# Streamed weight tiles moved by 64 bytes, and the dense layers rewritten in 256-column products

## Chip, cores and metric

The kernel runs on one core of one Trainium2 chip. The metric is the device time of one execution in microseconds (us). The median of three runs of the kernel before is 2948.8 us (2945.6 to 2950.67).

## What is computed

Two transformer blocks over 256 tokens of width 2048, in float32. Cut to what matters here:

```python
# first block
h = rmsnorm(x); proj = h @ w_in                      # 2048 -> 9264
y_a = y_pool @ w_pool_out;  y_b = (o_nsa * silu(g)) @ w_nsa_out
gm = sigmoid(h @ w_merge + b)
x = x + (gm[0] * y_a + gm[1] * y_b) @ w_out
# second block
z = rmsnorm(x) @ w_in_2                              # 2048 -> 6160
x = x + mixed @ w_out_2
# peer_ffn: 16384 experts, 8 heads of 16 chosen ones
q = xt @ w_q; idx, gate = top16(scores(q))
y = sum_k gelu(u[idx_k] . xt) * gate_k * v[idx_k]
```

The kernel computes the expert layer densely: it multiplies all 16384 rows of u with the tokens, multiplies the result by a matrix of gates that is zero for experts not chosen, and multiplies that by all of v. So every weight, 554 MB in all, is streamed through once.

## The kernel before, in words

Every large weight comes in blocks of 128 partitions x 1024 float32 (512 KB). `stream` (L178 is its DMA) loads a block into a ring tile wr, then `split` makes two float32r tiles of it: wh, a rounded copy, by ScalarE (L156), and wl, the remainder, by VectorE (L157). A product of full precision is then three products of parts: high x high, high x low and low x high. The activations are kept in the same way, in tiles S0 to S5 (class Parts): for each of 16 slices of 128 rows, 256 columns of high part and then 256 of low part, 2048 bytes.

TensorE does four kinds of large work, in this order in time:

- **Dense layers, weights stationary** (`dense_half`, 360 blocks, to 1372 us). A block holds eight slices k. For each, one 512-column product of wh with both parts of the activations (L209) writes 512 columns of PSUM, and one 256-column product of wl with the high part (L211; L208 at the end of a layer) is summed into the second half of those. A layer output of 128 rows is two blocks and takes a whole PSUM bank; its two halves are summed when it is taken out: `two_sums` copies the first half by ScalarE (L228) and adds the second by VectorE (L229). `pair_T` does this for two outputs and then multiplies by the norm's factor on GpSimd (L224). The three mm banks (`mmtile`) rotate.
- **Dense layers, weights moving** (`dense_N`, tile mmn, 64 blocks of 12 products of 512 columns, L190 to L192), between the former.
- **The expert layer up** (`dense_pair`, L1142, from 1386 to 2226 us). For 256 blocks of peer_u and 24 of w_pq, each block is 24 products of 256 columns, weights stationary, all summed into one place: eight of wh with the high part, eight of wh with the low part, eight of wl with the high part. After each block `work` issues small jobs from a list: the choice of experts (products sc) and, from about 1700 us, the gate matrix (products G, L1264).
- **The expert layer down** (`v_mm`, L1333 and L1337, from 2226 us). 256 blocks of peer_v, each 12 products of 512 columns, the streamed block moving and the gated activations ah and al stationary.

Where the tiles lie. Pools are laid out one behind the other in each partition. In the memory map of the kernel before, the constants start at a multiple of 128 bytes and take 5376 = 42 x 128 bytes, so the ring tiles wr, wh, wl of the pool "stream" (4096 bytes each) all start at a multiple of 128, and so do the S tiles (16640 = 130 x 128 bytes). Call such a tile aligned. The tile ypp (activations of w_po) starts 64 bytes past a multiple of 128, call that shifted. In the expert layer a second pool "stream2" is open, whose tiles are shifted, and so are ah and al. There `stream` takes wh and wl from stream2 for two blocks in five:

```python
        pl, nb = (more[0], more[2]) if more and turn[1] % 5 in (1, 3) else (ws, NHL)
```

In the pattern of five, then, blocks go shifted, aligned, shifted, aligned, aligned. S0 and S3 hold the activations of the expert layer up, S0 and S1 those of the first `dense_N`; S0, S2, S3 lie below 113 KB and S1, S4, S5 above, as stream2 does.

The order on each engine is that of a list scheduler in the tile framework, which works from the program's order and priorities. All weight DMAs are issued on SyncE's queue.

Of the kernel before, what the change touches and what calls it, by code (L numbers as in the profile page):

```python
# [7 lines left out]
F32 = mybir.dt.float32  # L8
F32R = mybir.dt.float32r
I32 = mybir.dt.int32  # L10
U32 = mybir.dt.uint32
AF = mybir.ActivationFunctionType
# [3 lines left out]
P = 128  # L16
T = 256
# [113 lines left out]
def emit(tc, I, out):  # L131
    nc = tc.nc
    ve, se, te, dma = nc.vector, nc.scalar, nc.tensor, nc.sync.dma_start
    mult, add, sub, amax = ALU.mult, ALU.add, ALU.subtract, ALU.max
    es = ExitStack()

    def pool(stack, name, bufs=1, psum=False, **kw):
        if psum:
            kw["space"] = bass.MemoryType.PSUM
        return stack.enter_context(tc.tile_pool(name=name, bufs=bufs, **kw))  # L140

    cp = pool(es, "const")
    ws = pool(es, "stream")

    def const(key, pl=None):
        ap = I[key]
        t = (pl or cp).tile(list(ap.shape), F32, name="k_" + key)
        dma(t, ap)
        return t
# [25 lines left out]
    def stream(src):  # L175
        n = src.shape[-1]
        r = raw_tile()
        dma(r[:, :n], src)  # L178
        turn[1] += 1
        pl, nb = (more[0], more[2]) if more and turn[1] % 5 in (1, 3) else (ws, NHL)  # L180
        h = pl.tile([P, 1024], F32R, tag="wh", bufs=nb, name="wh")
        l = pl.tile([P, 1024], F32R, tag="wl", bufs=nb, name="wl")
        on_pool[2] += 1
        eng = nc.gpsimd if on_pool[2] % on_pool[1] < on_pool[0] else ve
        split(r[:, :n], h[:, :n], l[:, :n], eng)
        return h, l
# [9 lines left out]
    def mmtile(name="mm"):  # L196
        return mm_pool[0].tile([P, 512], F32, tag="mm", bufs=mm_pool[1], name=name)
# [3 lines left out]
    def dense_half(pt, w, n, hf, x, start, stop):  # L201

        h, l = first.pop() if first else stream(w[n, hf])
        for k in range(8):
            kk, s = hf * 8 + k, slice(k * P, k * P + P)
            last = stop and k == 7
            if last:
                te.matmul(pt[:, T:], l[:, s], x.hi(kk), start=False, stop=False, skip_group_check=True)  # L208
            te.matmul(pt, h[:, s], x.both(kk), start=start and k == 0, stop=last, skip_group_check=True)  # L209
            if not last:  # L210
                te.matmul(pt[:, T:], l[:, s], x.hi(kk), start=False, stop=False, skip_group_check=True)  # L211
        if between:
            f, c = between.pop(0)
            f(c)

    def pair_T(dst, w, n2, x, r=None, nh=2):

        for a in range(2):
            pt = mmtile()
            for hf in range(nh):  # L220
                dense_half(pt, w, 2 * n2 + a, hf, x, hf == 0, hf == nh - 1)
            two_sums(dst[:, a], pt)
        if r is not None:
            nc.gpsimd.tensor_tensor(dst, dst, two(r), op=mult)  # L224
        return dst

    def two_sums(dst, pt):
        se.activation(dst, pt[:, :T], AF.Copy)  # L228
        ve.tensor_tensor(dst, dst, pt[:, T:], op=add)  # L229

    def dense_N(w, n, x):

# [10 lines left out]
    def two(r):  # L243
        return r[:, None, :].to_broadcast([r.shape[0], 2, T])

    sy = pool(es, "sy")
    es_x = ExitStack()
    sx = pool(es_x, "sx")
    SW = 4160
# [249 lines left out]
    pt = cmp_start("k")  # L499
# [3 lines left out]
    pt = cmp_start("v")  # L503
# [11 lines left out]
    h, l = stream(I["w_gb"])  # L515
    for k in range(KC):
        s = slice(48 * k, 48 * k + 48)
# [127 lines left out]

    es_m = ExitStack()
    pm = pool(es_m, "pm")
    ypp = Parts(pm.tile([P, 16 * T], F32R, name="ypp"))
    e8 = slice(0, 8)
    split(yp, ypp.hi(e8), ypp.lo(e8))  # L650
    on = parts(2, 4)
# [3 lines left out]
    mg = parts(5, 3)  # L655
    for n2 in range(8):
        g0, g1 = g0s[n2], g1s[n2]
        for g, w, x, nh in ((g0, "w_po", ypp, 1), (g1, "w_no", on, 2)):
            b = pair_T(pm.tile([P, 2, T], F32, tag="br", bufs=2, name="br"), I[w], n2, x, nh=nh)
            ve.scalar_tensor_tensor(g, g, 1.0, b, op0=add, op1=mult)  # L660
        ve.tensor_tensor(g0, g0, g1, op=add)
        ns = slice(2 * n2, 2 * n2 + 2)
        split_scaled(g0, 0.5, mg.hi(ns), mg.lo(ns))
        if n2 < 5:
            gate_pair(n2 + 3)
# [17 lines left out]
    pm = pool(es_m, "pm2")  # L683
# [3 lines left out]
    xr = act3(big(0, F32))  # L687
    for c in range(4):
        dma(xr[:, 4 * c:4 * c + 4], I["xT"][:, 4 * c:4 * c + 4])
    x1 = act3(big(1, F32))  # L690
# [1 line left out]
    acc1 = pm.tile([P, 2, T], F32, name="acc1")  # L692
    acc2 = pm.tile([P, 2, T], F32, name="acc2")
    for n2 in range(8):
        xs = pair_T(x1[:, 2 * n2:2 * n2 + 2], I["w_o"], n2, mg)
        nc.gpsimd.tensor_tensor(xs, xs, xr[:, 2 * n2:2 * n2 + 2], op=add)
        s1 = acc1 if n2 == 0 else pm.tile([P, 2, T], F32, tag="s1", bufs=2, name="s1")
        s2_ = acc2 if n2 == 0 else pm.tile([P, 2, T], F32, tag="s2", bufs=2, name="s2")
        for a in range(2):
            c = 2 * n2 + a  # L700
            split_scaled(xs[:, a], fn1[:, c:c + 1], zn.hi(c), zn.lo(c))
        se.activation(s1, xs, AF.Square)
        for a in range(2):
            c = 2 * n2 + a
            se.activation(s2_[:, a], xs[:, a], AF.Square, scale=fnw[:, c:c + 1])
        if n2:
            ve.tensor_tensor(acc1, acc1, s1, op=add)
            ve.tensor_tensor(acc2, acc2, s2_, op=add)
# [337 lines left out]

    def out_half(c, hf):
        if hf == 0:
            vs_[c] = mmtile()
        dense_half(vs_[c], I["w_o2"], c, hf, mx_, hf == 0, hf == 1)  # L1050

    for c in range(3):
# [1 line left out]
    for n2 in range(8):  # L1054
        xs = x1[:, 2 * n2:2 * n2 + 2]
        for c in (2 * n2, 2 * n2 + 1):
            if c > 2:
                out_half(c, 0)
            out_half(c, 1)
            v, xc = vs_.pop(c), x1[:, c]  # L1060
            for i in range(2):
                ve.tensor_tensor(xc, xc, v[:, T * i:T * i + T], op=add)
            split_scaled(xc, n2w[:, c:c + 1], x2.hi(c), x2.lo(c))
        s1 = acc3 if n2 == 0 else pc.tile([P, 2, T], F32, tag="s1", bufs=2, name="s1")
        se.activation(s1, xs, AF.Square)
        if n2:
            ve.tensor_tensor(acc3, acc3, s1, op=add)
        if n2 >= 2:
            to_rows(n2 - 2)
# [61 lines left out]
            f()  # L1131

    def dense_pair(pt, w, n2, rate):

        for a in range(2):
            o = pt[:, T * a:T * a + T]
            for hf in range(2):
                h, l = stream(w[2 * n2 + a, hf])
                for i in range(3):
                    for k in range(8):  # L1140
                        kk, s = hf * 8 + k, slice(k * P, k * P + P)
                        te.matmul(o, (l if i == 2 else h)[:, s], x2s.lo(kk) if i == 1 else x2s.hi(kk),  # L1142
                                  start=hf == 0 and i == 0 and k == 0, stop=hf == 1 and i == 2 and k == 7,
                                  skip_group_check=True)
                work(rate)

    def top16(src, vals, idx):
# [272 lines left out]
```

## Time and profile before

| | |
|---|---|
| median of three runs | 2948.8 us |
| the profiled execution, its own time | 2948.61 us |
| its span, first to last instruction | 2946.8 us |
| PE (TensorE matmul) busy | 2902.4 us, 98%, 17810 products |
| DVE (VectorE) busy | 1971.2 us, 67% |
| ACT (ScalarE) busy | 1595.7 us, 54% |
| POOL (GpSimd) busy | 152.2 us, 5% |
| mean DMA traffic | 202 GB/s |
| mean granted TensorE clock | 0.996 of 2.4 GHz |

How to read it: products are pipelined, so a product of 256 columns is shown as some 280 ns long while the next one starts after some 118 ns. What a product costs is read from start to start, not from its duration. A busy TensorE is therefore no measure of how fast its products follow one another. The sums below are made against the profiled execution; its time differs from the median by 0.2 us.

### The profile page before, as it was taken

The numbers are of one execution on the slowest core, as the hardware profiler recorded it, in microseconds if no ns is written. First come the engines' busy times: TensorE is split into PE (matmuls) and PEld (weight loads), VectorE is DVE, ScalarE is ACT, GpSimd is POOL, SyncE is SP. The second block draws the span as 40 slices with busy tenths as digits, with TensorE's granted clock in tenths as the row PEclk, the third lists the DMA queues.
The fourth block names the chain that finished last, engine by engine and source line by source line (L and its number), as shares of the span: only waits on it lengthen the run. The fifth ranks groups of instructions, "written<-read, shape, count | busy, mean of one in ns | idle before, by whom it ended". The sixth has DMA issues, their size and how long they took to land.

```text
span 2946.8 us, 46206 instructions
## 1 busy us (share of the span) xinstructions
PE 2902.4 (98%) x17810; PEld 2577.4 (87%) x17810; DVE 1971.2 (67%) x3127; ACT 1595.7 (54%) x2620; POOL 152.2 (5%) x145
## 2 busy tenths in 40 slices
PE   8999999999999999998999999999999999999998
PEld 6888888888888888887999999999998888888886
DVE  7775677766667776677787778888645555555554
ACT  5544555644455556555444479999644444444443
POOL 0010223300000000000000000000000000000000
PEclk9999999999999999999999999999999999999999
DMA  6756544565655555455656567677866776776753
GB/s 218 239 186 183 168 147 138 163 188 186 218 182 168 180 164 165 159 167 184 202 194 197 194 231 245 232 252 236 299 211 223 245 240 225 246 237 228 248 188 114
DMA packets 197181, 595.77 MB, mean 202 GB/s; under 512 B 20832, under 2 KB 55008, under 8 KB 192736
## 3 DMA queue, kind: packets, MB, share of 16 engines
q1 hardware_dynamic: 196960, 592.82, 61.8%
q8 instruction: 139, 2.28, 0.3%
q14 instruction: 82, 0.67, 0.1%
HBM read 553.92 MB, written 35.65 MB: 200 GB/s over the span
## 4 chain that ended last, share of the span: by engine, by line
PE 96%; DVE 2%; DMA 1%; ACT 1%; issue 0%; SPq 0%; DVEq 0%; ACTq 0%
PE mm L1142 25%; PE mm L209 22%; PE y L1333 16%; PE mm L211 11%; PE y L1337 8%; PE qp L1142 2%; PE mmn L191 2%; PE mmn L192 2%; PE mmn L190 2%; PE G L1264 1%; PE mm L208 1%; DVE wl L157 1%; DMA rsw<-rraw 1%; PE pT L605 1%; DMA wr<-in_w_kcr 1%; ACT wh L156 0%
## 5 line engine op out<-in xcount | busy, mean ns | idle before, releaser
L157 DVE TENSOR_TENSOR wl<-wr,wh 128x1024 fp32r<-128x1024 f32 x976 | 1225.5, 1258 | 719.1 <-ACT wh L156 693.9
L156 ACT ACTIVATE wh<-wr 128x1024 fp32r<-128x1024 f32 x976 | 1029.6, 1057 | 943.0 <-PE y L1333 364.5
L209 PE MATMUL mm<-S,wh 128*128 128x512 f32 x2752 | 973.5, 399 | 14.4 <-ACT wh L156 11.0
L211 PE MATMUL mm<-S,wl 128*128 128x256 f32 x2580 | 730.2, 283 | 3.9 <-DVE wl L157 3.8
L209 PEld LDWEIGHTS mm<-S,wh 128*128 128x128 f32 x2752 | 509.3, 188 | 121.0 <-ACT wh L156 13.0
L1142 PE MATMUL mm<-S,wh 128*128 128x256 f32 x4096 | 531.0, 282 | 0.0
L1142 PEld LDWEIGHTS mm<-S,wh 128*128 128x128 f32 x4096 | 506.3, 191 | 0.1
L211 PEld LDWEIGHTS mm<-S,wl 128*128 128x128 f32 x2580 | 488.4, 189 | 17.0 <-DVE wl L157 7.6
L1333 PE MATMUL y<-wh,ah 128*128 128x512 f32 x1008 | 315.0, 393 | 0.0
L1333 PE MATMUL y<-wh,al 128*128 128x512 f32 x1008 | 314.8, 393 | 0.0
L1142 PE MATMUL mm<-S,wl 128*128 128x256 f32 x2048 | 284.4, 282 | 0.0
L1337 PE MATMUL y<-wl,ah 128*128 128x512 f32 x1008 | 274.0, 392 | 0.0
L1142 PEld LDWEIGHTS mm<-S,wl 128*128 128x128 f32 x2048 | 261.1, 190 | 0.0
L1333 PEld LDWEIGHTS y<-wh,al 128*128 128x128 f32 x1008 | 188.8, 187 | 45.0
L1333 PEld LDWEIGHTS y<-wh,ah 128*128 128x128 f32 x1008 | 188.7, 187 | 44.4
L1337 PEld LDWEIGHTS y<-wl,ah 128*128 128x128 f32 x1008 | 188.8, 187 | 43.7
L191 PE MATMUL mmn<-wl,S 128*128 128x512 f32 x256 | 101.0, 394 | 3.3 <-DVE wl L157 3.3
L192 PE MATMUL mmn<-wh,S 128*128 128x512 f32 x256 | 100.6, 393 | 0.0
L190 PE MATMUL mmn<-wh,S 128*128 128x512 f32 x256 | 94.7, 394 | 0.0
L1262 ACT ACTIVATE om<-gm,gTl 128x128 fp32r<-128x128 f32 x256 | 93.3, 395 | 0.0
L1262 ACT ACTIVATE om<-gm,gTh 128x128 fp32r<-128x128 f32 x256 | 87.0, 395 | 0.2 <-DVE gm L1254 0.2
L1268 ACT ACTIVATE gst<-G 128x256 f32<-128x256 f32 x128 | 80.7, 634 | 2.2
(484 smaller groups left out, 2581.0 us busy)
## 6 DMA issues: line engine op xcount, KB each, us to landing
wr<-in_peer_u SPq DMA_DIRECT2D x256, 512.0 KB, 4.2
wr<-in_peer_v SPq DMA_DIRECT2D x256, 512.0 KB, 4.3
wr<-in_w_mg SPq DMA_DIRECT2D x64, 512.0 KB, 3.5
wr<-in_w_o SPq DMA_DIRECT2D x64, 512.0 KB, 3.5
wr<-in_w_q SPq DMA_DIRECT2D x32, 512.0 KB, 4.0
wr<-in_w_gn SPq DMA_DIRECT2D x32, 512.0 KB, 3.5
wr<-in_w_no SPq DMA_DIRECT2D x32, 512.0 KB, 3.6
wr<-in_w_pq SPq DMA_DIRECT2D x32, 512.0 KB, 3.5
```

Of the source, the lines that this page charges most:

```text
L156: se.activation(hi, src, AF.Copy)
L157: (eng or ve).tensor_tensor(lo, src, hi.bitcast(F32), op=sub)
L190: te.matmul(out_, ah, bh, start=start, stop=False, skip_group_check=True)
L191: te.matmul(out_, ah, bl, start=False, stop=False, skip_group_check=True)
L192: te.matmul(out_, al, bh, start=False, stop=stop, skip_group_check=True)
L209: te.matmul(pt, h[:, s], x.both(kk), start=start and k == 0, stop=last, skip_group_check=True)
L211: te.matmul(pt[:, T:], l[:, s], x.hi(kk), start=False, stop=False, skip_group_check=True)
L1142: te.matmul(o, (l if i == 2 else h)[:, s], x2s.lo(kk) if i == 1 else x2s.hi(kk), start=hf == 0 and i == 0 and k == 0, stop=hf == 1 and i = ...
L1262: se.activation(om[:, t, P * i:P * i + P], o2[:, t], AF.Copy, scale=gt.bitcast(F32)[:, tk + t:tk + t + 1])
L1268: se.activation(g2, pt[:, :, 0], AF.Copy)
L1333: te.matmul(yb[tt, c + d], a[p][:, ts], w[0][d], start=i == 0 and p == 0, stop=False, **f)
L1337: te.matmul(yb[tt, c + d], a[0][:, ts], w[1][d], start=False, stop=i == P - 1, **f)
```

## The change

- A tile of 16 float32 (64 bytes) is laid at the start of the pool "stream", and another at the start of the pool of S0, S2 and S3. The ring tiles of "stream" become shifted, and everything from S0 on moves by 128 bytes and keeps its place against a multiple of 128. The tile ypp starts 16 elements later and becomes aligned. GpSimd clears the two pads once.
- `dense_half` issues 24 products of 256 columns per block, in the order of `dense_pair`, all summed into 256 columns. Two outputs share a bank (`pair_P`).
- An output pair is taken out by one operation of 512 columns: a copy by ScalarE, or VectorE's product with the norm's factor, or the operation that used to follow it (L660 for w_po and w_no, L696 for w_o, now on VectorE). `two_sums`, the GpSimd products L224 and the tile br go. The two additions of L1062 become one.
- `dense_pair` calls `dense_half`; its products and their order stay.

```diff
+    pad = ws.tile([P, 16], F32, name="pad")
+    nc.gpsimd.memset(pad, 0.0)
...
     def dense_half(pt, w, n, hf, x, start, stop):
         h, l = first.pop() if first else stream(w[n, hf])
-        for k in range(8):
-            kk, s = hf * 8 + k, slice(k * P, k * P + P)
-            last = stop and k == 7
-            if last:
-                te.matmul(pt[:, T:], l[:, s], x.hi(kk), start=False, stop=False, skip_group_check=True)
-            te.matmul(pt, h[:, s], x.both(kk), start=start and k == 0, stop=last, skip_group_check=True)
-            if not last:
-                te.matmul(pt[:, T:], l[:, s], x.hi(kk), start=False, stop=False, skip_group_check=True)
+        for i in range(3):
+            for k in range(8):
+                kk, s = hf * 8 + k, slice(k * P, k * P + P)
+                te.matmul(pt, (l if i == 2 else h)[:, s], x.lo(kk) if i == 1 else x.hi(kk),
+                          start=start and i == 0 and k == 0, stop=stop and i == 2 and k == 7, skip_group_check=True)
...
+    def pair_P(w, n2, x, nh=2):
+        pt = mmtile()
+        for a in range(2):
+            for hf in range(nh):
+                dense_half(pt[:, T * a:T * a + T], w, 2 * n2 + a, hf, x, hf == 0, hf == nh - 1)
+        return pt.rearrange("p (a t) -> p a t", a=2)
+
     def pair_T(dst, w, n2, x, r=None, nh=2):
-        for a in range(2):
-            pt = mmtile()
-            for hf in range(nh):
-                dense_half(pt, w, 2 * n2 + a, hf, x, hf == 0, hf == nh - 1)
-            two_sums(dst[:, a], pt)
-        if r is not None:
-            nc.gpsimd.tensor_tensor(dst, dst, two(r), op=mult)
+        pt = pair_P(w, n2, x, nh)
+        if r is None:
+            se.activation(dst, pt, AF.Copy)
+        else:
+            ve.tensor_tensor(dst, pt, two(r), op=mult)
         return dst
...
     sy = pool(es, "sy")
+    pad2 = sy.tile([P, 16], F32, name="pad2")
+    nc.gpsimd.memset(pad2, 0.0)
...
-    ypp = Parts(pm.tile([P, 16 * T], F32R, name="ypp"))
+    ypp = Parts(pm.tile([P, 16 * T + 16], F32R, name="ypp")[:, 16:])
...
-            b = pair_T(pm.tile([P, 2, T], F32, tag="br", bufs=2, name="br"), I[w], n2, x, nh=nh)
-            ve.scalar_tensor_tensor(g, g, 1.0, b, op0=add, op1=mult)
+            ve.scalar_tensor_tensor(g, g, 1.0, pair_P(I[w], n2, x, nh), op0=add, op1=mult)
...
-        xs = pair_T(x1[:, 2 * n2:2 * n2 + 2], I["w_o"], n2, mg)
-        nc.gpsimd.tensor_tensor(xs, xs, xr[:, 2 * n2:2 * n2 + 2], op=add)
+        xs = x1[:, 2 * n2:2 * n2 + 2]
+        ve.tensor_tensor(xs, pair_P(I["w_o"], n2, mg), xr[:, 2 * n2:2 * n2 + 2], op=add)
...
-            vs_[c] = mmtile()
+            vs_[c] = mmtile()[:, :T]
...
-            for i in range(2):
-                ve.tensor_tensor(xc, xc, v[:, T * i:T * i + T], op=add)
+            ve.tensor_tensor(xc, xc, v, op=add)
```

## Rows read from the trace of the kernel before

**Rows 1.** The page: engines' busy time; the chain that ended last, by engine.

```profile
PE 2902.4 (98%) x17810; PEld 2577.4 (87%) x17810; DVE 1971.2 (67%) x3127; ACT 1595.7 (54%) x2620; POOL 152.2 (5%) x145
...
PE 96%; DVE 2%; DMA 1%; ACT 1%; issue 0%; SPq 0%; DVEq 0%; ACTq 0%
```

**Rows 2.** Busy time of each engine by stretch (columns: stretch, length, engines, PEclk, DMA, GB/s).

```profile
600.00:840.00 240.00, 240.00 (x1366) 208.91 (x1365) 149.97 (x167) 116.61 (x166) 12.86 (x10) 1.00 0.61 196
...
1700.00:2100.00 400.00, 400.00 (x3388) 400.00 (x3388) 313.49 (x423) 351.85 (x810) 0.00 (x0) 1.00 0.70 240
...
2230.00:2900.00 670.00, 670.00 (x2898) 542.49 (x2897) 376.86 (x417) 289.32 (x304) 0.00 (x0) 1.00 0.71 231
```

**Rows 3.** Line 209's products by what they read: duration min/median/max, first and last start.

```profile
L209 PE MATMUL mm<-S,wh x2752: 387/395/796, 7.5 to 1372.1; 128*128 128x512 f32 x197
...
L209 PE MATMUL mm<-ypp,wh x128: 388/394/398, 597.0 to 833.1; 128*128 128x512 f32 x128
```

**Rows 4.** Timeline of PE, expert layer up: starts of the wh products of consecutive blocks.

```profile
1538.64 2.05 PE L1142 MATMUL mm<-S,wh 128*128 128x256 f32 x16
...
1541.47 2.08 PE L1142 MATMUL mm<-S,wh 128*128 128x256 f32 x16
...
1544.35 2.05 PE L1142 MATMUL mm<-S,wh 128*128 128x256 f32 x16
...
1547.17 2.08 PE L1142 MATMUL mm<-S,wh 128*128 128x256 f32 x16
...
1550.06 2.08 PE L1142 MATMUL mm<-S,wh 128*128 128x256 f32 x16
```

**Rows 5.** The same timeline where gate products G stand between blocks.

```profile
1804.20 2.08 PE L1142 MATMUL mm<-S,wh 128*128 128x256 f32 x16
...
1807.08 0.64 PE L1264 MATMUL G<-om,ah 128*128 128x256 f32 x4
1807.56 1.98 PE L1142 MATMUL mm<-S,wh 128*128 128x256 f32 x16
...
1810.28 2.08 PE L1142 MATMUL mm<-S,wh 128*128 128x256 f32 x16
...
1853.88 2.05 PE L1142 MATMUL mm<-S,wh 128*128 128x256 f32 x16
...
1856.70 1.48 PE L1142 MATMUL mm<-S,wh 128*128 128x256 f32 x11
```

**Rows 6.** Timeline of PE, expert layer down: the first products of consecutive blocks.

```profile
2301.15 0.63 PE L1333 MATMUL y<-wh,ah 128*128 128x512 f32 x2
...
2303.95 0.62 PE L1333 MATMUL y<-wh,ah 128*128 128x512 f32 x2
...
2306.69 0.63 PE L1333 MATMUL y<-wh,ah 128*128 128x512 f32 x2
```

**Rows 7.** Timeline of PE, first dense_N layer: starts of blocks 1, 2, 5 and 6.

```profile
233.13 0.62 PE L190 MATMUL mmn<-wh,S 128*128 128x512 f32 x2
...
235.86 0.61 PE L190 MATMUL mmn<-wh,S 128*128 128x512 f32 x2
...
246.73 0.62 PE L190 MATMUL mmn<-wh,S 128*128 128x512 f32 x2
...
249.45 0.62 PE L190 MATMUL mmn<-wh,S 128*128 128x512 f32 x2
```

**Rows 8.** Groups by line: what takes a pair out, and a 512-column VectorE read of PSUM.

```profile
L229 DVE TENSOR_TENSOR g<-g,mm 128x256 f32<-128x256 f32 x32 | 13.4, 418 | 20.0 <-ACT g L228 20.0
...
L228 ACT ACTIVATE g<-mm 128x256 f32<-128x256 f32 x32 | 12.2, 380 | 41.1 <-PE mm L209 41.0
```

```profile
L161 DVE SCALAR_TENSOR_TENSOR fv<-mmn,rzn,fv x4: 750/751/752, 1061.6 to 1196.7; 128x512 fp32r<-128x512 f32 x4
```

**Rows 9.** Who waited for whom, PE's own: total us, times, longest.

```profile
PE sc L190 <- ACT kyh L156: 12.5, 1, 12.5
PE mm L209 <- ACT wh L156: 11.0, 2, 7.5
PE mm L211 <- DVE wl L157: 3.8, 8, 0.8
```

More of the change, by code (lines that the diff above doesn't have):

```diff
@@ L214, in dense_half @@
             f(c)
-    def pair_T(dst, w, n2, x, r=None, nh=2):
-        for a in range(2):
-            pt = mmtile()
-            for hf in range(nh):
-                dense_half(pt, w, 2 * n2 + a, hf, x, hf == 0, hf == nh - 1)
-            two_sums(dst[:, a], pt)
-        if r is not None:
-            nc.gpsimd.tensor_tensor(dst, dst, two(r), op=mult)
-        return dst
-    def two_sums(dst, pt):
-        se.activation(dst, pt[:, :T], AF.Copy)
-        ve.tensor_tensor(dst, dst, pt[:, T:], op=add)
+    def pair_P(w, n2, x, nh=2):
[4 more added lines that the diff above has]
+        return pt.rearrange("p (a t) -> p a t", a=2)
+    def pair_T(dst, w, n2, x, r=None, nh=2):
+        pt = pair_P(w, n2, x, nh)
[3 more added lines that the diff above has]
+            ve.tensor_tensor(dst, pt, two(r), op=mult)
+        return dst
     def dense_N(w, n, x):
@@ L1135, in dense_pair @@
         for a in range(2):
-            o = pt[:, T * a:T * a + T]
             for hf in range(2):
[L1138 to L1144, printed above, removed]
+                dense_half(pt[:, T * a:T * a + T], w, 2 * n2 + a, hf, x2s, hf == 0, hf == 1)
                 work(rate)
```

## The prediction, made before the change was run

> **What bounds the kernel.** I began with the page's engine totals and its chain of waits: TensorE is busy 98% of the span, and 96% of the chain that ended last is TensorE following itself [rows 1]. Its waits add up to little, of which 12.5 us stand at one place, 11.0 and 3.8 in the dense layers [rows 9]. So the time is a sum of products from start to start, and a change that touches every product has to be priced by that. The view by stretch gives averages (stretch divided by count), the timeline the single blocks. In the stretch from 600 to 840 us, dense layers alone, 1366 products are 683 steps of 512 + 256 columns, so 0.351 us per step and 2.81 us per block of eight [rows 2]. Elsewhere, next to attention and at the starts of layers, blocks of up to 2.9 us stand in the timeline; I take 2.82 us as the mean of a block that doesn't wait. There are (2752 + 128) / 8 = 360 of them [rows 3].
>
> **What a block costs by its place.** Blocks of the expert layer up, all alike except for the ring they came from, start 2.83, 2.88, 2.82 and 2.89 us apart in turn [rows 4], in just the order in which the ring alternates shifted and aligned tiles. So 24 products of 256 columns cost 2.88 us aligned and 2.83 us shifted. Where another product has stood in between, an aligned block still takes 2.88 (1804.20 to 1807.08), while a shifted one mostly falls to 2.72 us (1807.56 to 1810.28), though not always: 2.82 from 1853.88 to 1856.70 [rows 5]. Over the whole stage, by the starts of all products, I count 24 of 32 such shifted blocks that settle at about 113.3 ns per product, the others at 117.9; without a product in between, 9 of 80. Within a block the level, once reached, stays. An aligned block never gets below 2.84. Moving 512-column blocks behave the other way round: against the shifted stationary ah, al an aligned block takes 2.80 us (2301.15 to 2303.95) and a shifted one 2.74 (2303.95 to 2306.69) [rows 6]; against the aligned stationary S an aligned block takes 2.73 and 2.72 [rows 7]. Blocks 1 and 5 of that layer read S0 and S1, which lie in quite different parts of the memory, and cost the same; so it is the place against 128 bytes and not the part of the memory that I take to decide. In short, 256-column products like the two operands 64 bytes apart, 512-column ones like them equal.
>
> **Part 1, expert layer up.** 280 blocks, of which 168 are aligned. Now: 168 x 2.88 + 112 x 2.81 (the mean of the shifted ones) = 798.5 us. After, all are shifted: between 280 x 2.72 = 761.6 and 280 x 2.83 = 792.4. Which of the two levels holds is the unknown. Entered from an aligned block it is the slow one; after an interruption it was the fast one 3 times in 4; and with no aligned blocks left, nothing pulls it back but the next interruption. I take 3/4 fast: 2.75 us, 770 us, **-28.5 us**; ends -37 and -6.
>
> **Part 2, dense layers.** After the change their blocks are what a shifted block of part 1 is: the same 24 products in the same order, weights shifted, activations aligned (ypp too, after its 16 elements). 360 x (2.75 - 2.82) = **-25 us**; ends 360 x (2.72 - 2.82) = -36 and 360 x (2.83 - 2.82) = +4.
>
> **Part 3, expert layer down.** 154 of 256 blocks were aligned, and become shifted: 154 x (2.74 - 2.80) = **-9 us**. If blocks that follow one another shifted also lose the slower products at their start, the level in them (12 x 226.7 ns = 2.72 us) would give -14; that is the other end, and 0 is the poorest I allow.
>
> **Part 4, dense_N.** Here the change works against itself: its blocks become shifted against aligned S, 64 bytes apart, as the 2.80 us blocks of the down layer are now. 64 x (2.80 - 2.72) = +5 at most, since some blocks already take 2.80; I take **+3 us**, ends 0 and +5.
>
> **Part 5, taking out.** A pair cost two ScalarE copies of 380 ns and two VectorE additions of 418 ns [rows 8], then mostly a product on GpSimd. Now it costs one operation, which I price by VectorE's 512-column read of PSUM at 751 ns [rows 8]. Both engines have room in the dense stretch: VectorE 150 of 240 us, ScalarE 117 of 240 [rows 2]. TensorE needs three banks; a bank now fills in four blocks (some 11 us) where two filled it before, so 0.75 us for emptying it is hidden with two banks to spare. Without that cover it would be 86 pairs x 0.75 = 65 us. VectorE's in-order queue holds the next wl split, of which each block needs one, behind that operation for 0.75 us, shorter than the 0.84 us it spent before on the same pair. GpSimd's queue loses the products and nothing waits behind the two pads, which are cleared before the first load has landed. No DMA is moved in the program; each queue runs ahead by ring slots as before. **0 us**, ends -3 and +5.
>
> **Part 6, waits.** The waits for wl (3.8 us) should mostly go, as wl is first read 16 products after wh; **-1 us**, ends -4 and +4. The 12.5 us wait at 1372 us [rows 9] hangs on VectorE's and ScalarE's work on S0 and S3 that starts when the last layer's norm is known; TensorE reaches it 8 blocks x 0.07 = 0.6 us sooner after that start and waits that much longer. The 11.0 us at the start are the first loads; they stay.
>
> **Sum:** -28.5 - 25 - 9 + 3 + 0 - 1 = -60.5, so 2948.6 - 60.5 = 2888 us, which is also what I predict against the median, 0.2 us higher.
>
> **A rule against it.** The trace says that a block's place in the memory changes its time by 0.05 to 0.16 us [rows 4, 5]. The Trainium skill, page "SBUF — State Buffer", section "SBUF: two separate sides", says that TensorE never waits for anyone at the memory, by which a shift of 64 bytes would be worth nothing. Its page "TensorE: Matmul & The Clock Gate", section "Back-to-back issue gap", gives each product its columns at 2.4 GHz plus about 2.5 ns; an estimate from that is 2880 products more x 2.5 ns = +7 us for the dense layers and 0 elsewhere, 2956 us.
>
> **Rivals.**
> - *The shift does nothing* (the rings differ for another reason). Then dense blocks become what unshifted 256-column blocks are, 2.88 us [rows 4]: 360 x (2.88 - 2.82) = +22, all else unchanged, 2970 us: slower. It decides if the first dense blocks take over 2.82 us. For it: shift and ring can't be told apart within the expert layer. Against it: rows 7, where the part of the memory did nothing, and rows 6, where the ring that is slower with one partner is the faster kind with another. The rule above is of this kind. Chance 0.06.
> - *The slow shifted level holds nearly everywhere.* Then +4 - 6 - 9 + 5 = -6, 2942 us; with a quarter to a half of the blocks fast, 2925 to 2905. For it: 80 uninterrupted shifted blocks, 71 of them slow [rows 4]. Against it: each of these came straight from an aligned block. Chance 0.18, most of it in the upper half of what it can gain.
> - *ScalarE becomes the bound while the gate matrix is made.* From 1700 to 2100 us it is busy 352 of 400 us [rows 2]; at 2.75 us a block the same work has 386 us, 91%, and a late wh stops TensorE. If that stretch gains nothing, part 1 loses 14 us: 2902 us. Chance 0.08.
> - The forecast itself, with half or more of the blocks at the fast level: 2864 (all fast, part 3 at -14) to 2905 (half). Chance 0.68.
>
> **Numbers.** Predicted 2888 us. The range 2862 to 2932 holds the forecast, the ScalarE case and two thirds of the slow level; the flat rival and the rest stay out. A measurement of this kernel can tell about 0.2%, 6 us. Faster by more: the forecast, ScalarE's case and four fifths of the slow level, 0.90; within: 0.04; slower: 0.06.
>
> **What would show it.** In the changed kernel's timeline: dense blocks of 24 products 2.72 or 2.83 us apart and never 2.88; no alternation by ring in the up and down layers, the down layer at 2.72 to 2.74; dense_N at 2.80; products per 100 us in the up layer near 870 against 847 now [rows 2]; PE's waits still under 50 us in all. I am wrong if dense blocks take 2.88, if a new wait of more than 10 us stands behind a bank or a wh, or if the down layer keeps 2.80.

## The result, and the profile after

The changed kernel takes 2918.6 us (median of four, 2918.2 to 2920.7) beside 2949.0 for the kernel before: a ratio of 0.990, 95% interval 0.988 to 0.992. It is faster, by 30.4 us. That is inside the range, but half of the forecast 60.5. The profiled execution took 2919.0 us with a span of 2917.2; the span before was 2946.8, so 29.6 us went. The page's totals and chain, the answer to [rows 1]:

```profile
PE 2879.9 (99%) x20690; PEld 2690.4 (92%) x20690; DVE 1896.0 (65%) x2994; ACT 1563.2 (54%) x2463; POOL 80.7 (3%) x92
...
PE 97%; DVE 1%; DMA 1%; ACT 1%; issue 0%; SPq 0%; DVEq 0%; ACTq 0%
```

TensorE still bounds it, with 2880 products more in a shorter time. Busy time by stretch, the columns as in [rows 2]:

```profile
600.00:840.00 240.00, 239.45 (x2034) 239.25 (x2032) 127.02 (x125) 103.26 (x113) 0.00 (x0) 1.00 0.56 196
...
1700.00:2100.00 400.00, 400.00 (x3451) 400.00 (x3451) 317.99 (x409) 356.23 (x817) 0.00 (x0) 1.00 0.72 250
2230.00:2880.00 650.00, 650.00 (x2817) 528.43 (x2816) 367.54 (x406) 282.90 (x296) 0.00 (x0) 1.00 0.65 228
```

In the dense stretch a product takes 240 / 2034 = 118.0 ns, so a block of 24 takes 2.83 us; it was 2.81. The up layer gained (3451 products in 400 us against 3388). The down layer hardly did: 650 / 2817 = 230.7 ns against 231.2. The granted clock is 1.00 in all of them. So the difference is not the clock.

Now the blocks. The timeline of PE in the dense layers, starts of successive wh products (columns: start, duration, engine, line, operation, tiles, shape, count):

```profile
624.47 2.05 PE L210 MATMUL mm<-S,wh 128*128 128x256 f32 x16
626.35 1.10 PE L210 MATMUL mm<-S,wl 128*128 128x256 f32 x8
627.29 2.05 PE L210 MATMUL mm<-S,wh 128*128 128x256 f32 x16
...
1000.05 1.98 PE L210 MATMUL mm<-S,wh 128*128 128x256 f32 x16
1001.86 1.07 PE L210 MATMUL mm<-S,wl 128*128 128x256 f32 x8
1002.77 1.98 PE L210 MATMUL mm<-S,wh 128*128 128x256 f32 x16
```

The first block takes 2.82 us (117.8 ns a product), the later one 2.72 (113.3). Both are shifted blocks of the same kind, and the operands of both lie at the same distance from one another. The same timeline in dense_N, the answer to [rows 7], then in the up layer among gate products, to [rows 5], and in the down layer, to [rows 6]:

```profile
232.55 0.63 PE L193 MATMUL mmn<-wh,S 128*128 128x512 f32 x2
...
235.35 0.63 PE L193 MATMUL mmn<-wh,S 128*128 128x512 f32 x2
...
1808.00 0.63 PE L1258 MATMUL G<-om,ah 128*128 128x256 f32 x4
1808.47 2.05 PE L210 MATMUL mm<-S,wh 128*128 128x256 f32 x16
1810.35 1.10 PE L210 MATMUL mm<-S,wl 128*128 128x256 f32 x8
1811.29 1.99 PE L210 MATMUL mm<-S,wh 128*128 128x256 f32 x16
1813.12 1.07 PE L210 MATMUL mm<-S,wl 128*128 128x256 f32 x8
1814.03 0.63 PE L1258 MATMUL G<-om,ah 128*128 128x256 f32 x4
...
2300.78 0.62 PE L1327 MATMUL y<-wh,ah 128*128 128x512 f32 x2
...
2303.57 0.63 PE L1327 MATMUL y<-wh,ah 128*128 128x512 f32 x2
...
2306.30 0.62 PE L1327 MATMUL y<-wh,ah 128*128 128x512 f32 x2
```

The up layer's pair after G takes 2.82 and 2.74 us; no block takes the 2.88 of [rows 4]. The down layer still alternates, 2.79 and 2.73, although all its blocks are now shifted like ah. dense_N takes 2.80 us.

What took out a pair [rows 8] and the waits of PE [rows 9] afterwards:

```profile
L230 DVE TENSOR_TENSOR g<-mm,r 128x512 f32<-128x512 f32 x16 | 11.1, 691 | 20.0 <-PE mm L210 20.0
L663 DVE SCALAR_TENSOR_TENSOR g<-g,mm 128x512 f32<-128x512 f32 x16 | 11.0, 689 | 21.7 <-PE mm L210 21.7
```

```profile
PE sc L193 <- ACT kyh L159: 11.0, 1, 11.0
PE mm L210 <- ACT wh L159: 9.3, 2, 7.8
PE mxT L1009 <- DVE fo L1008: 2.5, 1, 2.5
PE cmp L194 <- DVE wl L160: 1.7, 2, 1.0
...
PE mm L210 <- DVE g L663: 0.9, 1, 0.9
```

The one operation takes 0.69 us. PE waits behind such an operation once, 0.9 us at 840 us (the last line); before the change it waited as long there, for L229. All PE waits together fell from 34.6 to 28.1 us.

**Where the time went**, by the trace's starts of products: the time from each start to the next, added up by kind, waits included.

| us | dense | dense_N | up | down | other |
|---|---|---|---|---|---|
| before | 1050.6 | 181.7 | 799.4 | 710.6 | 187.0 |
| after | 1045.7 | 183.0 | 775.7 | 709.2 | 186.1 |
| difference | -4.9 | +1.3 | -23.7 | -1.4 | -0.9 |
| forecast | -25 | +3 | -28.5 | -9 | 0 (and -1 for waits) |

Of the 31 us that are missing against the forecast, 20 lie in the dense layers, 8 in the down layer and 5 in the up layer; dense_N gave 2 back.

### The profile page after: what moved, and what is told of

It reads as the page before. It is cut to its first block, busy times and chain, and to the rows that moved or that the text cites. A ratio compares the mean times of both kernels' runs of the same rounds, so it can differ in the third digit from the quotient of the medians.

```text
span 2917.2 us, 51579 instructions
## 1 busy us (share of the span) xinstructions
PE 2879.9 (99%) x20690; PEld 2690.4 (92%) x20690; DVE 1896.0 (65%) x2994; ACT 1563.2 (54%) x2463; POOL 80.7 (3%) x92
## 4 chain that ended last, share of the span: by engine, by line
PE 97%; DVE 1%; DMA 1%; ACT 1%; issue 0%; SPq 0%; DVEq 0%; ACTq 0%
PE mm L210 58%; PE y L1327 16%; PE y L1331 8%; PE qp L210 2%; PE mmn L194 2%; PE mmn L195 2%; PE mmn L193 2%; PE G L1258 1%; PE pT L609 1%; DMA wr<-in_w_kcr 0%; PE po L193 0%; PE po L194 0%; DVE kb L405 0%; PE po L195 0%; ACT wh L159 0%
## 5 line engine op out<-in xcount | busy, mean ns | idle before, releaser
L160 DVE TENSOR_TENSOR wl<-wr,wh 128x1024 fp32r<-128x1024 f32 x976 | 1191.6, 1223 | 777.0 <-ACT wh L159 719.2
L210 PE MATMUL mm<-S,wh 128*128 128x256 f32 x9600 | 1243.3, 280 | 11.2 <-ACT wh L159 9.3
L210 PEld LDWEIGHTS mm<-S,wh 128*128 128x128 f32 x9600 | 1173.6, 188 | 16.7 <-ACT wh L159 10.6
L210 PE MATMUL mm<-S,wl 128*128 128x256 f32 x4800 | 664.4, 279 | 0.0
L210 PEld LDWEIGHTS mm<-S,wl 128*128 128x128 f32 x4800 | 604.4, 188 | 1.8 <-issue 1.0
L599 POOL TENSOR_SCALAR sm<-sm,ls 128x128 f32<-128x128 f32 (+1 forms) x64 | 77.4, 1225 | 272.5 <-DVE sc L595 143.6
L1263 DVE TENSOR_TENSOR gst<-gst,G 128x256 f32<-128x256 f32 x128 | 76.7, 634 | 2.7 <-ACT gst L1262 2.5
L194 PEld LDWEIGHTS mmn<-wl,S 128*128 128x128 f32 x256 | 48.2, 188 | 11.7 <-DVE wl L160 1.4
L195 PEld LDWEIGHTS mmn<-wh,S 128*128 128x128 f32 x256 | 48.2, 188 | 10.6
```

Source lines behind the costliest of these rows:

```text
L160: (eng or ve).tensor_tensor(lo, src, hi.bitcast(F32), op=sub)
L194: te.matmul(out_, ah, bl, start=False, stop=False, skip_group_check=True)
L195: te.matmul(out_, al, bh, start=False, stop=stop, skip_group_check=True)
L210: te.matmul(pt, (l if i == 2 else h)[:, s], x.lo(kk) if i == 1 else x.hi(kk), start=start and i == 0 and k == 0, stop=stop and i == 2 and ...
L599: nc.gpsimd.tensor_scalar(v, v, ls[:, c:c + 1], None, op0=mult)
L1263: ve.tensor_tensor(g2, g2, pt[:, :, 1], op=add)
```

## The experiments

Below, a block's *distance* is its place less that of the operand it meets, counted against 256 bytes, from the memory map of each kernel. After the change, blocks of the first ring have distance 192 to S (64 bytes before it) and 64 to ypp, and those of stream2 64 to S (64 bytes behind it). A *run* is a row of 256-column products with no other product and no wait in it, counted by its times from start to start; in the dense layers there are 110 of more than eleven, the longest of 2403 (556 to 839 us in the changed kernel). *Fast* is 113.3 ns a product, *slow* 117.8; the *fast share* of the tables is the share of the dense layers' times from start to start that are under 115.5 ns. The columns by stage come from one traced execution each, and the time in front of them is a median: the trace of e4 was 5.7 us faster than its median and that of e13 3.3 slower, so a few us in one column decide nothing.

**The two halves apart, and the ring staggered.** e1 is the changed kernel without its shifts, e2 the kernel before with the shifts alone, in e3 the slots of the first ring are 128 bytes longer, and in e4 stream2 and ah stand 128 bytes further.

```diff
 e1 (undone)                                   e3
-    pad = ws.tile([P, 16], ...)              +        wide = 1056 if pl is ws else 1024
-    pad2 = sy.tile([P, 16], ...)             +        h = pl.tile([P, wide], F32R, tag="wh", ...)
-    ypp = ...[P, 16 * T + 16] ...[:, 16:]     e4
+    ypp = ...[P, 16 * T] ...                 +    pad3 = more[0].tile([P, 32], F32, name="pad3")
```

> The changed kernel with its three shifts taken back (both pads and the 16 elements of ypp): the dense layers stay in 256-column products, now aligned. Theory (256-column products cost about 120 ns aligned, and 113.3 or 117.8 ns shifted): dense and up-layer products all at 119 to 120 ns from start to start; the up layer goes back from 776 us to 799 us, the dense layers (8640 products) rise by 8640 x 3 ns = 26 us; in all 2965 to 2972 us, slower than both kernels. Rival (the shift does nothing, the gain is that of fewer operations for taking out): within 5 us of the changed kernel, 2914 to 2924 us.

> The kernel before with only the shifts added; dense layers in 512 + 256 columns and everything taken out as before. Theory (the gain is the address, and it is made in the up layer): the up layer falls from 799 to about 776 us as in the changed kernel; the dense layers change by -8 to +3 us; 2918 to 2930 us. Rival (the 256-column form of the dense layers carries its own share): the dense layers stay where they were or get slower, and the total stays over 2930 us.

> The changed kernel with ring tiles of the pool stream 128 bytes wider, so that neighbouring ring slots lie alternately 64 and 192 bytes past a multiple of 256; all stay 64 past a multiple of 128. Theory A (a step of 128 bytes in the weights' place between blocks lets the products out of the slow level, 117.8 ns, into the fast one, 113.3 ns, as the trace shows in the up layer when a block of stream2 follows one of stream): the dense layers, now at 117 ns on the mean, fall to 113.3 to 115 ns, 8640 x 2.0 to 3.7 ns = 17 to 32 us; the up layer gains 0 to 10 us; the down layer 0 to 5 us; 2875 to 2901 us. Rival B (which level holds is settled only by interruptions, other products or waits): dense layers still 116.5 to 117.5 ns, 2911 to 2922 us.

> The changed kernel with a tile of 128 bytes ahead of the pool stream2: its tiles and all tiles behind them, ah and al too, move by 128 bytes; blocks of both rings then lie alike against 256 bytes, and alike with ah and al. Theory (512-column products are fast, 226.7 ns, where moving and stationary operand lie alike against 256 bytes, not against 128): all blocks of the down layer at 2.72 to 2.74 us instead of three in five at 2.79, that is -8 to -12 us. And by theory A of the stagger run the up layer loses the steps of 128 bytes that led it to the fast level: 115.1 ns rise to 116 to 117.8 ns, +6 to +18 us; total 2912 to 2926 us. By rival B the up layer stays at 115 ns, total 2906 to 2911 us. If the place against 128 bytes alone mattered, the down layer would stay at 709 us.

| | us (ratio, 95% interval) | dense | fast share | up | down |
|---|---|---|---|---|---|
| e1 | 2965.9 (1.004 to 1.007) | 1071.9 | 0.00 | 799.4 | 710.6 |
| e2 | 2927.1 (0.991 to 0.994) | 1052.5 | - | 775.8 | 709.2 |
| e3 | 2895.1 (0.980 to 0.983) | 1030.3 | 0.75 | 774.3 | 703.9 |
| e4 | 2907.3 (0.985 to 0.988) | 1042.4 | 0.28 | 774.2 | 696.4 |

Without the shifts, the dense layers in 256-column form take 21 us longer than before the change. Their blocks then take 2.88 us, as the timeline of PE in e1 shows:

```profile
620.41 2.08 PE L207 MATMUL mm<-S,wh 128*128 128x256 f32 x16
622.33 1.12 PE L207 MATMUL mm<-S,wl 128*128 128x256 f32 x8
623.29 2.08 PE L207 MATMUL mm<-S,wh 128*128 128x256 f32 x16
```

The shifts alone give the dense layers nothing (+2) and the up layer all of its gain. So in the dense layers the two depend on each other. e4 settles the down layer: with every block at distance 0 but for the last 48 products, it takes 226.8 ns a product, as its stretch shows (columns as before):

```profile
2250.00:2850.00 600.00, 600.00 (x2649) 496.82 (x2648) 345.96 (x384) 264.46 (x277) 0.00 (x0) 1.00 0.70 236
```

After the change the first ring's blocks were at distance 128 from ah: equal against 128 bytes, and not against 256. In e3 runs that began slow turned fast in the middle, at a step of the ring's place; all 31 such turns in the changed kernel stand at steps too. From that came the theory that a step lifts a run. The trace of e3 also shows the opposite, which the theory leaves out: 14 times a row of dense products at 113.3 ns fell to 117.8 at the start of a block. e4, without steps, had been expected to lose in the up layer by that theory; it did not.

**Is 64 special, and does the step do it?** e5 doubles both pads, e6 halves the first (and fills up the second). e7 needs no pads: slots are 1088 floats wide, and the block's place in its slot follows its use (dense and up alternately at distance 64 and 192, dense_N and down at 0). e8 is e7 without the alternation, always 64.

```diff
 e5 / e6
-    pad = ws.tile([P, 16], ...);  pad2 = sy.tile([P, 16], ...)
+    pad = ws.tile([P, 32], ...);  pad2 = sy.tile([P, 32], ...)      (e6: 8 and 24)
 e7 / e8
+    PLACE_WS = {"d": (16, 48), "n": (0, 0), "v": (16, 16)}           (e8: "d": (16, 16))
-        h = pl.tile([P, 1024], F32R, tag="wh", ...)
+        h = pl.tile([P, 1088], F32R, tag="wh", ...)[:, o:o + 1024]
```

> Pads twice as large: the weights of the first ring now stand 128 bytes from the activations (counted against 256 bytes), those of the second ring 64; nothing else changes. If the 256-column products see the distance against 128 bytes, the dense blocks go back to some 120 ns a product as without pads (dense layers near 1072 us), the expert layer up to about 3/5 of its blocks at 120 and 2/5 at 113 to 118, so 795 to 800 us, and the whole to 2950 to 2970 us. If any distance other than 0 against 256 is good, dense products stay at 113 to 118 ns and the whole near 2915. The down layer, whose first-ring blocks now stand 64 from ah against 256, should be as before the change, 710 us.

> First pad halved: the weights of the first ring stand 32 bytes past a place equal to the activations' (against 128 bytes, 96 or 32 by direction) instead of 64. If 64 is special because it is the farthest from equal, dense products lie between 113 and 120 ns, and the whole between 2918 and 2965 us; if any distance is as good, the whole stays at 2918 within 10 us; if 32 is bad like 0, near 2955 to 2966 us.

> No pads; each streamed block's place inside its slot is chosen by its use: dense and up blocks alternately 64 and 192 bytes from the activations (against 256), dense_N blocks and the down layer's equal to their partner. By the theory that 256-column products have two levels at distance 64 against 128, and that a step of the place by 128 bytes lifts the slow one to the fast one: dense near 1025 us, up 770 to 775, the down layer at 226.7 ns a product, 696 us, dense_N 176 to 179 us; whole 2860 to 2885 us. By the rival that the step did nothing and the staggered run's gain came from other places of the tiles: dense near 1045, whole near 2900.

> The same as the kernel with places by use, but dense and up blocks always 64 bytes from the activations, without the alternation. By the theory of the step: dense 1040 to 1048 us as after the change, the down layer 696 and dense_N 176 to 179 as in its twin, up 772 to 785; whole 2890 to 2905 us, 15 to 30 us above its twin. By the rival, that the step is nothing, both are equal within 6 us.

| | us (ratio, 95% interval) | dense | fast share | up | down |
|---|---|---|---|---|---|
| e5 | 2946.3 (one run) | 1064.3 | 0.16 | 788.3 | 707.1 |
| e6 | 2965.7 (one run) | 1070.2 | 0.04 | 793.5 | 713.9 |
| e7 | 2882.3 (0.976 to 0.979) | 1024.2 | 0.78 | 774.9 | 696.1 |
| e8 | 2887.6 (0.978 to 0.981) | 1027.5 | 0.78 | 776.7 | 696.1 |

A distance of 32 against 128 is as poor as 0 (e6, 119.7 ns in the longest run); 128 is nearly so (e5, 119.0 ns there). The 0.16 of e5 is no fast level: it is single products of 115 ns among others of 117 to 122, and no run of its dense layers holds 113.3. The theory of the step fell with e8: no step, and the dense layers are as fast as with it. What e8 has in common with e7 and not with the changed kernel is distance 64 instead of 192, weights 64 bytes *behind* the activations instead of before them.

**The side.** e9 is the changed kernel with pads of 192 bytes (first ring at distance 64, ypp moved along); e10 is e8 on the other side, 192; in e11 wh stands at 64 and wl at 192, so that the place steps twice in each block.

```diff
 e9
-    pad = ws.tile([P, 16], ...);  pad2 = sy.tile([P, 16], ...);  ypp = ...16 * T + 16] ...[:, 16:]
+    pad = ws.tile([P, 48], ...);  pad2 = sy.tile([P, 48], ...);  ypp = ...16 * T + 48] ...[:, 48:]
 e10 (from e8)
-    PLACE_WS = {"d": (16, 16), ...    PLACE_2 = {"d": (0, 0), ...
+    PLACE_WS = {"d": (48, 48), ...    PLACE_2 = {"d": (32, 32), ...
 e11 (from e8)
+        o = (48 if pl is ws else 32) if use == "d" else o            (between h and l)
```

> The changed kernel with both pads three times as large (192 bytes) and ypp aligned with S: against 256 bytes the weights of both rings stand 64 after the activations (in the changed kernel the first ring stood 64 before them), dense_N's too, and the down layer's blocks equal to ah. If the side decides how often a dense run takes the fast level, dense 1025 to 1032 us; the down layer 696 us by the rule of equal places against 256; dense_N 179 to 184; up 772 to 778; whole 2882 to 2895 us. By the rival that the side does nothing and the gain of the kernel with places by use came from the absolute places or from chance, dense stays at 1042 to 1048 and the whole at 2900 to 2908.

> The kernel with places by use and no alternation, but dense and up blocks 64 bytes before the activations (against 256) instead of 64 after them. If the side decides, dense goes from 1027 to 1040 to 1048 us and the whole to 2900 to 2910; the down layer stays at 696 and dense_N at 179. By the rival, that the side does nothing, the whole stays at 2888 within 6 us.

> The kernel with places by use, with wh 64 bytes after the activations and wl 64 bytes before them in every block, so that the place steps by 128 bytes twice in each block. If a step lifts a run from the slow level to the fast one, no run stays slow for more than a block: up 762 to 770 us (from 775 to 777), dense 1018 to 1024, whole 2866 to 2880 us. If the step does nothing, 2888 within 6 us; if steps can lower the level as well, 2890 to 2905.

| | us (ratio, 95% interval) | dense | fast share | up | down |
|---|---|---|---|---|---|
| e9 | 2884.8 (0.977 to 0.980) | 1023.9 | 0.81 | 778.5 | 696.5 |
| e10 | 2923.7 (0.989 to 0.993) | 1049.9 | 0.16 | 793.4 | 696.1 |
| e11 | 2908.7 (0.985 to 0.988) | 1043.6 | 0.33 | 782.7 | 696.1 |

Both sides came out as the theory of the side had it for the dense layers, a little beyond it at both ends (1023.9 and 1049.9). The stretches of e9, the columns as before:

```profile
600.00:840.00 240.00, 239.13 (x2110) 238.96 (x2110) 133.79 (x133) 107.84 (x121) 0.00 (x0) 1.00 0.60 202
...
1700.00:2100.00 400.00, 400.00 (x3448) 400.00 (x3447) 312.75 (x400) 348.48 (x794) 0.00 (x0) 1.00 0.74 254
2250.00:2850.00 600.00, 600.00 (x2649) 496.82 (x2648) 344.75 (x380) 265.80 (x278) 0.00 (x0) 1.00 0.69 230
```

and of e10:

```profile
600.00:840.00 240.00, 240.00 (x2040) 240.00 (x2039) 127.46 (x125) 103.01 (x113) 0.00 (x0) 1.00 0.58 196
...
1700.00:2100.00 400.00, 400.00 (x3404) 400.00 (x3403) 312.84 (x410) 353.12 (x812) 0.00 (x0) 1.00 0.71 243
```

In the dense stretch e9 issues 2110 products where e10 issues 2040 and the changed kernel 2034. The run of 2403 products is fast from its first block to its last in e8 and e9, and slow throughout in the changed kernel, e4 and e10. Not every run follows the side: the next longest, of 766, is slow in the changed kernel and fast in e4, and fast in e9 and slow in e13 (below), though within each pair the dense layers' tiles lie alike. That is 3.4 us, and what sets the beginning of this run stays open.

e11 took longer than any of its three forecasts. A step, by e11, lifts a run from the slow level only sometimes: 14 times in 303 steps from 192 to 64, against 31 in 39 in the changed kernel's up layer; and those 14 all stand near a run's beginning: of the steps with 16 or more products of the run before them, none of 271 in e11 lifted it, but 31 of 38 in the changed kernel. No step from 64 to 192 did it in either. What decides that stays open.

The up layer of e10 had not been expected to lose 17 us. In e4 it was fast half the time at the same distance of 192. What differs between them is where G's operands om and oj stand against S: 64 in e10, 192 in e4.

**The interrupting products.** e12 adds to e9 a pad of 128 bytes at the head of the pool with om, oj, ah, al. e13 instead moves om and oj alone, inside wider slots, and leaves ah and al; e14 moves only om (the moving operand).

```diff
 e12
+        pad3 = pv[0].tile([P, 32], F32, name="pad3")
 e13 / e14
+    def slot(pl, tag, name, o):
+        t = pl.tile([P, 2 * T + 64], F32R, tag=tag, bufs=GRP // 2 + 1, name=name)
+        return t[:, o:o + 2 * T].rearrange("p (a t) -> p a t", a=2)
+            om = slot(pv[0], "al", "om", 32)
+        oj = slot(pv[0], "ah", "ah", 32)                              (e14: 0)
```

> The kernel with pads of 192 bytes, and one pad of 128 bytes more at the head of the pool that holds the gate operands om, ah, al, so that these stand 192 against 256 while both rings stay at 64 and S at 0. Of the up layer's 62 runs of products that follow a gate product G, 31 were fast in the kernel without this pad. If the level after an interruption follows the streamed block's place against the operands of the interrupting product (equal: half fast, 128 apart: none), now none or nearly none of the 62 is fast and the up layer takes 790 to 796 us instead of 778; if it follows the side to S alone, about 31 remain and the layer stays at 775 to 780. Either way the down layer, its blocks 128 from ah, goes from 696 to 715 us or so (233 ns a product, by the rule of places against 256), and the dense layers stay at 1024. Whole 2912 to 2922 us by the first, 2898 to 2908 by the second.

> The kernel with pads of 192 bytes, with om and oj (both operands of the gate products G) placed 128 bytes further inside wider slots; ah and al of the down layer stay where they were. If the places of G's operands decide the level of the runs that follow them, all 62 are fast as with the third pad (31 without), the up layer takes 766 us instead of 778, and the down layer keeps 696: whole 2868 to 2878 us. If something else that the third pad moved decided (gst, gm, the pool's other tiles), 31 stay fast, up 778, whole 2881 to 2890.

> The same, but om alone (the moving operand of G) 128 bytes further, oj where it was. If the moving operand decides, as in the kernel with both moved: 62 of 62 fast, up 766, whole 2868 to 2878 us. If the stationary operand oj decides, 31 of 62, up 778, whole 2881 to 2890. If both count, something between.

| | us (ratio, 95% interval) | dense | up | fast after G | down |
|---|---|---|---|---|---|
| e12 | 2893.6 (0.980 to 0.984) | 1023.5 | 765.9 | 62 of 62 | 713.5 |
| e13 | 2876.7 (0.974 to 0.977) | 1030.9 | 766.1 | 62 of 62 | 696.5 |
| e14 | 2885.3 (0.977 to 0.980) | 1022.7 | 776.8 | 31 of 62 | 696.5 |

e12 went the opposite way to the theory it was made for: every run after G was fast, not none. The down layer lost what was expected (its blocks at distance 128 again, 232.3 ns a product). The stretches of e12:

```profile
1700.00:2100.00 400.00, 400.00 (x3510) 400.00 (x3509) 313.40 (x399) 349.47 (x790) 0.00 (x0) 1.00 0.75 257
2250.00:2850.00 600.00, 600.00 (x2584) 486.43 (x2583) 337.38 (x372) 258.78 (x271) 0.00 (x0) 1.00 0.67 226
```

3510 products in 400 us are 114.0 ns, with G among them. Its timeline shows the fast pairs right behind G, 2.74 and 2.72 us:

```profile
1806.43 0.64 PE L1260 MATMUL G<-om,ah 128*128 128x256 f32 x4
1806.91 1.99 PE L210 MATMUL mm<-S,wh 128*128 128x256 f32 x16
1808.74 1.07 PE L210 MATMUL mm<-S,wl 128*128 128x256 f32 x8
1809.65 1.98 PE L210 MATMUL mm<-S,wh 128*128 128x256 f32 x16
1811.46 1.07 PE L210 MATMUL mm<-S,wl 128*128 128x256 f32 x8
1812.37 0.64 PE L1260 MATMUL G<-om,ah 128*128 128x256 f32 x4
```

e13 shows that it is G's operands and nothing else in that pool, and e14 that the moving one alone does nothing. That oj alone would do it was not tried. Put together, the 62 runs that follow a G, by the place of the run's weights and of oj, both against S:

| weights | oj | fast | kernels |
|---|---|---|---|
| 64 | 192 | 62 of 62 | e12, e13 |
| 64 | 64 | 31 of 62 | e8, e9, e14 |
| 192 | 192 | 31 of 62 | e4 |
| 192 | 64 | 0 of 62 | e10 |

In the changed kernel both cases with oj at 64 stand side by side: 14 of 26 runs at 64, 0 of 36 at 192. The half in 31 of 62 is not chance: in e4, e8, e9 and e14 it is every second run, in strict turn, in e4 those that are slow in the other three. What also returns with every second gate job is the pair of PSUM banks that G writes (`side_bank` goes through four, two per job; oj and om go through five slots). That the bank decides is not shown: no run moved it. e13 is the fastest kernel of the study: 2876.7 us, 42 us less than the changed one, for pads and places alone.

## Why the prediction was right or wrong

- **What bounds it**: right. TensorE follows itself in 97% of the chain.
- **Part 1, up layer**, -28.5: measured -23.7, the mechanism right in part. No block takes 2.88 any more, no row of products at 113.3 ns fell back before the next interruption, and 0.63 of the products are fast where 3/4 was taken. But only 14 of 62 runs after G began fast; 31 rows at 117.8 ns were lifted at a step from the first ring to stream2, which the forecast did not have, so that 0.63 comes near 3/4 is partly luck. The 24 of 32 counted in the trace of before were blocks of stream2, at distance 64 [rows 5]; 168 of the 280 came to stand at 192, where no run after G began fast. "All are shifted" treated the two sides as one. e12 and e13, at 0.94 fast, reach -33.
- **Part 2, dense layers**, -25: wrong, and the step that failed is "their blocks are what a shifted block of part 1 is", with 3/4 of them fast. Measured: 0.19 fast, 2.807 us a block without its waits against 2.8125 before, so about -2 us, and some 3 us less of waits. Without a step of the weights a run keeps the level that it takes in its first block (so every dense run of a block or more in the traces of the changed kernel, e4, e8 to e10 and e12 to e14), and a few beginnings decide much: two, of 2403 and 766 products, both at 117.8 ns, hold 37% of all dense products. The share came from runs behind G in another stage; the dense layers' runs follow other products, and their weights stood on the other side of S. With the side alone changed (e9 against the changed kernel, e8 against e10) 22 us come, about what part 2 had promised.
- **Part 3, down layer**, -9: wrong, measured -1.4. The step that failed is "it is the place against 128 bytes and not the part of the memory that I take to decide". For 512-column products it is against 256: 226.7 ns at distance 0, 233 at 128 and 192, 230 at 64. Before the change, the fast kind had distance 0 and the slow 192 [rows 6], so no row of before could tell 128 from 256. "If the down layer keeps 2.80" was named as a sign of error, and came for the first ring's blocks: 2.79.
- **Part 4, dense_N**, +3: right. Blocks at 2.80 as forecast; 234.6 against 229.4 ns are +4.0 us over 768 products, of which shorter waits gave back 2.7.
- **Part 5, taking out**, 0: right. 0.69 us instead of the 0.75 taken, one wait of 0.9 us behind it as before the change, GpSimd's work halved at no gain.
- **Part 6, waits**, -1: the sign was right, the size -6.5 us over all of PE's waits, outside the end of -4. Those of the dense layers for wl (3.8) are gone as said; the one at kyh, said to grow by 0.6, fell from 12.5 to 11.0, and the first loads' from 11.0 to 9.3.
- **The rivals.** "The shift does nothing" is out: e1 against the changed kernel is 47 us, and its +22 for the unshifted dense layers was +21.3. The rule cited with it (the Trainium skill, "SBUF — State Buffer", section "SBUF: two separate sides", by which TensorE never waits for anyone at the memory) speaks of waiting for others and not of an engine's own two operands; it doesn't give these times: the same products took 120 ns at one distance and 113.3 or 117.8 at others. The +7 us estimated from the Trainium skill, "TensorE: Matmul & The Clock Gate", section "Back-to-back issue gap", is not seen either: at their best places two products of 256 columns (2 x 113.3) take just what one of 512 takes (226.7). "The slow shifted level holds nearly everywhere" is what came in the dense layers, though not in the up layer; its "with a quarter to a half of the blocks fast, 2925 to 2905" holds the total, at a chance of 0.18, but by another split (0.19 of the products fast in the dense layers, 0.63 in the up layer). ScalarE did not become the bound: at 3510 products per 400 us (e12) it was busy 349 us and stopped nobody.

So the total was wrong for two main reasons of about 20 and 8 us, in parts 2 and 3, both of one kind: a rule read off two cases was carried to places where its cases did not reach.

## What to carry to other kernels

When like products differ in time by the place of their operands, tabulate the time by the distance of the two operands modulo 256 bytes at the least, with its sign, before choosing a pad; then place each tile by its use, as slots a little wider allow (e7, e8). Where a level persists until an interruption, don't forecast by the share of products that were fast, but by the runs: how long they are, and what each of them begins behind. One long run can hold the whole gain.

## What was not expected of the hardware

- 256-column float32r products have two stable levels with the same operands, 113.3 and 117.8 ns, at distances 64 and 192, one of which holds over 2403 products (272 us or 283); at distance 0 they take 120.
- Which level a run takes depends on the places of the products *before* it: 31 or 62 of 62 runs fast at distance 64, and 0 or 31 at 192, by 128 bytes in the place of an interrupting product's stationary operand or of both its operands; where it is 31, it is every second run.
- 512-column products have their best at distance 0, where 256-column ones have their worst: 226.7 ns.
- Why there are two levels, and why a step of 128 bytes lifts a run in one kernel and hardly ever in another, the runs do not show.
